# Six of eleven gate-and-up blocks as seven block products, the FFN width in three parts

## The chip, the cores and the metric

The kernel runs on one core of one Trainium2 chip. The metric is device time in microseconds for one execution; a figure for a kernel is the median of its runs. TensorE (PE) multiplies, VectorE (DVE) and ScalarE (ACT) do the elementwise work, GpSimd (POOL) a little of it, and SyncE (SP) issues most of the DMAs.

## The reference

One decoder block for 256 tokens of width 2048, all in float32:

```python
h = h + hybrid_mixer(rmsnorm(h, mix_norm_w), w_in, ...)   # projections, gated linear attention, short conv, w_out
h = h + swiglu(rmsnorm(h, ffn_norm_w), w_gate_up, w_down)
return rmsnorm(h, final_norm_w)

def swiglu(h, w_gate_up, w_down):
    gu = jnp.einsum('bsd,df->bsf', h, w_gate_up)
    gate, up = jnp.split(gu, [FFN_HIDDEN], axis=-1)        # FFN_HIDDEN = 5632
    return jnp.einsum('bsf,fd->bsd', jax.nn.silu(gate) * up, w_down)
```

Only the second line, the FFN, is computed differently by the change.

## The kernel before

Tokens stand in two tiles `t` of 128. The contraction over 2048 is cut into 16 chunks of 128 (`KC`). Weights come as a stream of pieces of 128 x 1024 elements (512 KB): for an output of 512 columns a piece holds two chunks. `load_piece` (L112) handles one: a DMA on SP into `raw` (L127), a cast on ACT into the rounded part `hi` (L128), and a subtraction on DVE, `lo = raw - hi` (L129). Each of the three has six buffers, and `take` (L144) keeps `LOOK` = 5 pieces loaded ahead of the one in use. Activations are split in the same way into `xh`, `xl` (later `hh`, `hl` and `acth`, `actl`). `mm3` (L154) makes a product of full accuracy from three matmuls: hi·lo (L156), lo·hi (L157), hi·hi (L158). A piece so gives 2 chunks x 2 token tiles x 3 = 12 matmuls of 128x128 by 128x512 (`tok_piece`, `mm_tok`). All output goes through six rotating PSUM banks (`pmm`) and two auxiliary ones (`pax`).

[...] Small jobs are put between the pieces by `later(n, fn)`, which runs `fn` after `n` more pieces.

The FFN has 11 blocks `f` of 512 hidden columns. A block takes eight pieces of the gate matrix (`fg`) and eight of the up matrix (`fu`), 192 matmuls; its gate goes through a sigmoid on ACT (L637) and a product on DVE (L638), the up part through another product (L642), and both token tiles of the result are transposed on PE (L276) and split into `acth`, `actl` (L278, L279). The width is worked in two halves, blocks 0 to 5 and 6 to 10; after each half, the down products (`dn`) of its blocks go into four or five column groups and are added to `h` (L661). The output projection (`wo`) stands ahead of the FFN; with each of its four column groups `h` is transposed, multiplied by the norm's gain and split into `hh`, `hl` (`transpose_gain`, L264 to L269). After the last down product, `finish` scales and stores each token tile.

Of the kernel before, what the change touches and what calls it, by code (L numbers as in the profile page):

```python
# [15 lines left out]
P = 128  # L16
# [27 lines left out]
def plan():  # L44
    """Every weight group in the order of its use: (key, matrix, first row, row chunks, first column, columns)."""
# [14 lines left out]
    for half, (f0, f1) in enumerate(HALVES):  # L60
# [3 lines left out]
        for n, (c0, w) in enumerate(DOWN[half]):  # L64
            groups.append((f"dn{half}_{n}", "w_dn", f0 * 512, (f1 - f0) * 4, c0, w))
# [3 lines left out]
HALVES = ((0, 6), (6, 11))  # L69
DOWN = (  # L70
    ((0, 512), (512, 512), (1024, 512), (1536, 512)),
    ((0, 512), (512, 512), (1024, 512), (1536, 256), (1792, 256)),
)


def piece_list():
    """The groups cut into pieces of PIECE elements per partition; the first two groups alternate."""
    out = []
    for key, mat, r0, nk, c0, w in plan():
        n = PIECE // w  # L80
        out.append([(key, mat, r0 + k * P, k, min(n, nk - k), c0, w) for k in range(0, nk, n)])
    first = [p for pair in zip(out[0], out[1]) for p in pair]
    return first + [p for g in out[2:] for p in g]


@with_exitstack
def block_kernel(ctx, tc, x, xt, cols_in, gkw_in, gku_in, gnw, conv_w, finw, w_in, w_out, w_gu, w_dn, out):
# [5 lines left out]
    wraw = ctx.enter_context(tc.tile_pool(name="wraw", bufs=6))  # L93
    whi = ctx.enter_context(tc.tile_pool(name="whi", bufs=6))
    wlo = ctx.enter_context(tc.tile_pool(name="wlo", bufs=6))
# [3 lines left out]
    pmm = ctx.enter_context(tc.tile_pool(name="pmm", bufs=6, space=bass.MemoryType.PSUM))  # L99
    pax = ctx.enter_context(tc.tile_pool(name="pax", bufs=2, space=bass.MemoryType.PSUM))  # L100
# [4 lines left out]
    stream = piece_list()  # L105
    at_matrix = {}
# [3 lines left out]
    pending = []  # L110

    def load_piece():  # L112
        i = count["loaded"]
        count["loaded"] += 1
        key, mat, _, k0, n, _, w = stream[i]
        j = at_matrix.get(mat, 0)
        at_matrix[mat] = j + 1
        raw = wraw.tile([P, n, w], F32, tag="raw", name="raw")
        hi = whi.tile([P, n, w], F32R, tag="hi", name="hi")
        lo = wlo.tile([P, n, w], F32R, tag="lo", name="lo")  # L120
        # the first piece in two parts, so that the products begin sooner
        step = n // 2 if i == 0 else n
        for a in range(0, n, step):
            b = a + step
            if (i, a) in hooks:
                hooks.pop((i, a))()
            nc.sync.dma_start(raw[:, a:b, :], mats[mat][j, :, a * w:b * w].rearrange("p (k c) -> p k c", c=w))  # L127
            nc.scalar.copy(hi[:, a:b, :], raw[:, a:b, :])  # L128
            nc.vector.tensor_tensor(out=lo[:, a:b, :], in0=raw[:, a:b, :], in1=hi[:, a:b, :].bitcast(F32),  # L129
                                    op=ALU.subtract)  # L130
        ready[(key, k0)] = (hi, lo, n)

    def later(delay, fn):
        """Run fn once `delay` more pieces have been used."""
        pending.append((count["tick"] + delay, fn))

    def tick():
        count["tick"] += 1
        due = [p for p in pending if p[0] <= count["tick"]]
        for p in due:  # L140
            pending.remove(p)
            p[1]()

# [10 lines left out]
    def mm3(ps, sh, sl, mh, ml, first, last):  # L154
        """ps += (sh + sl).T @ (mh + ml) without the product of the two low parts."""
# [4 lines left out]
    def tok_piece(ps, t, piece, k0, nk, ah, al):  # L160
        hi, lo, n = piece
        ts = slice(t * P, (t + 1) * P)
        for k in range(n):
            kk = k0 + k
            mm3(ps, ah[:, kk, ts], al[:, kk, ts], hi[:, k, :], lo[:, k, :], kk == 0, kk == nk - 1)

    def mm_tok(key, nk, w, ah, al):
        """Token-major product: out[t] = a[:, t].T @ w, with a's chunks stationary."""
        ps = [pmm.tile([P, w], F32, tag="mm", name=f"{key}_{t}") for t in range(NT)]
        for k0 in range(0, nk, PIECE // w):  # L170
            piece = take(key, k0)
            for t in range(NT):
                tok_piece(ps[t], t, piece, k0, nk, ah, al)
# [11 lines left out]
    def mm_cols(keys, ah, al, each=None):  # L185
        """Column-major products: out[m] = w[:, m].T @ a, with w's chunks stationary."""
        ps = {key: [pmm.tile([P, T], F32, tag="mm", name=f"{key}_{m}") for m in range(2)] for key in keys}
# [8 lines left out]
    # ---------------------------------------------------------------- constants  # L196
# [3 lines left out]
    warm = const.tile([P, 512], mybir.dt.bfloat16, name="warm")  # L200
# [4 lines left out]
    warm_ps = pax.tile([P, 512], F32, tag="ax", name="warm_ps")  # L205
# [3 lines left out]
    mix = ExitStack()  # L209
    mpool = mix.enter_context(tc.tile_pool(name="mpool", bufs=1))  # L210
    gla = ExitStack()
    gpool = gla.enter_context(tc.tile_pool(name="gpool", bufs=1))

    # the low-rank decay's down-projection: hi in columns 0:16, lo in 16:32 of one stationary operand
# [4 lines left out]
    # ---------------------------------------------------------------- x: split of x * gain, transposed  # L219
# [22 lines left out]
    # x arrives in step with the first pieces of the weights  # L242
# [7 lines left out]
    # ---------------------------------------------------------------- helpers  # L250
# [8 lines left out]
    def transpose_gain(c0, hi, lo):  # L259
        """Chunks c0, c0 + 1 of h to hi + lo = (h * gain) transposed."""  # L260
        ps = pax.tile([P, 2, T], F32, tag="ax", name="tr")
        for j in range(2):
            for t in range(NT):
                nc.tensor.transpose(out=ps[:, j, t * P:(t + 1) * P],  # L264
                                    in_=h[:, t, (c0 + j) * P:(c0 + j + 1) * P], identity=ident)
        for j in range(2):
            c = c0 + j
            nc.scalar.activation(hi[:, c, :], ps[:, j, :], AF.Copy, scale=ffc[:, c:c + 1])
            nc.vector.scalar_tensor_tensor(out=lo[:, c, :], in0=ps[:, j, :], scalar=ffc[:, c:c + 1],  # L269
                                           in1=hi[:, c, :].bitcast(F32), op0=ALU.mult, op1=ALU.subtract)  # L270

    def transpose_block(src, t, hi, lo, c0):
        """128 tokens x 512 columns to four chunks of hi + lo."""
        ps = pax.tile([P, 4, P], F32, tag="ax", name="trb")
# [7 lines left out]
    # ---------------------------------------------------------------- first products  # L282
    gk_ps = pax.tile([P, T], F32, tag="ax", name="gk_ps")
# [10 lines left out]
    mask = const.tile([P, NT, P], I8, name="mask")  # L294
    restart = const.tile([P, T], F32, name="restart")
# [3 lines left out]
    rb = const.tile([P, T], F32, name="rb")  # L299
# [12 lines left out]
    def make_constants():  # L312
# [3 lines left out]
        # mask[j, i] = 1 where j <= i, for both token tiles  # L316
        maskf = const.tile([P, P], F32, name="maskf")
# [410 lines left out]
```

## Time and profile before

| what | us |
|---|---|
| median of 3 runs (1563.91 to 1564.59) | 1564.22 |
| span of the profiled execution | 1561.5 |
| PE busy in it | 1549.7 |
| DVE busy | 859.3 |
| ACT busy | 706.4 |
| first matmul of the output projection | 732.6 |
| first gate product | 823.3 |
| first down product | 1089.9 |
| last matmul begins | 1553.7 |

The span runs from the first to the last instruction of the profiled execution; the time of a run also holds what lies around it. Busy times of PE are modelled and overlap, so the distance of the starts of two matmuls, not the duration of one, says what a matmul costs. In rows of groups, the numbers behind the bar are the total of busy time, the mean duration in ns, and the idle time of the engine just before them with what ended it.

### The profile page before, as it was taken

Reading aid. Unit: us, or ns where it says so; the run is one execution under the profiler, and the core shown is the slowest. Engines: PE = TensorE matmul, PEld = TensorE weight load, DVE = VectorE, ACT = ScalarE, POOL = GpSimd, SP = SyncE. Lnnn points to the kernel's source line nnn. Section 1 sums busy time; section 2 is a strip of 40 time slices with the busy share of each in tenths; the row PEclk is TensorE's granted clock in tenths of the full one; section 3 lists DMA queues with packets and bytes.
Section 4 is the critical chain, followed back from the end, with each engine's and each line's share of the span. In section 5 each row is a group of like instructions: output and inputs, shape, how many; then the busy total and the mean of one; then the engine's idle time right before and its main releaser. Section 6 shows DMA issues by size and latency. Waiting matters only on the chain.

```text
span 1561.5 us, 18914 instructions
## 1 busy us (share of the span) xinstructions
PE 1549.7 (99%) x7417; PEld 1304.0 (84%) x7417; DVE 859.3 (55%) x866; ACT 706.4 (45%) x797; POOL 16.6 (1%) x29
## 2 busy tenths in 40 slices
PE   9999999999999999999999999999999999999998
PEld 8989988888888888888888888888888888888887
DVE  6765546554745655665555555555544555555554
ACT  7763453444444344444445444444433444444443
POOL 0020000000000000000000000000000000000000
PEclk9999999999999999999999999999999999999999
DMA  9655567766766766666566666565666666666561
GB/s 351 208 171 170 179 194 206 231 189 204 231 191 190 242 192 190 201 213 193 188 183 215 188 190 191 189 192 189 188 192 197 190 189 189 189 195 188 189 197 68
DMA packets 86081, 306.11 MB, mean 196 GB/s; under 512 B 9740, under 2 KB 9868, under 8 KB 85864
## 3 DMA queue, kind: packets, MB, share of 16 engines
q1 hardware_dynamic: 82560, 296.02, 60.0%
q10 hardware_dynamic: 3432, 8.89, 2.3%
q8 instruction: 58, 0.95, 0.3%
q14 instruction: 31, 0.25, 0.0%
HBM read 298.60 MB, written 2.10 MB: 193 GB/s over the span
## 4 chain that ended last, share of the span: by engine, by line
PE 96%; DVE 1%; ACT 1%; issue 1%; POOL 0%; DMA 0%; SPq 0%; DVEq 0%; ACTq 0%
PE dn L158 5%; PE dn L157 5%; PE dn L156 5%; PE fg L158 5%; PE fg L156 5%; PE fg L157 5%; PE fu L158 5%; PE fu L156 5%; PE fu L157 5%; PE wo L158 2%; PE gc L156 2%; PE g L156 2%; PE gb L156 2%; PE xc L156 2%; PE wo L157 2%; PE ma L156 2%
## 5 line engine op out<-in xcount | busy, mean ns | idle before, releaser
L129 DVE TENSOR_TENSOR lo<-raw,hi 128x1024 fp32r<-128x1024 f32 (+1 forms) x553 | 674.5, 1223 | 629.6 <-ACT hi L128 629.2
L128 ACT CAST hi<-raw 128x1024 fp32r<-128x1024 f32 (+1 forms) x553 | 579.7, 1051 | 780.2 <-PE fu L158 140.0
L156 PE MATMUL dn<-lo,acth 128*128 128x512 f32 (+1 forms) x392 | 144.2, 368 | 0.0
L158 PE MATMUL dn<-hi,acth 128*128 128x512 f32 (+1 forms) x392 | 144.0, 367 | 0.0
L157 PE MATMUL dn<-hi,actl 128*128 128x512 f32 (+1 forms) x392 | 144.0, 367 | 0.0
L156 PE MATMUL fg<-lo,hh 128*128 128x512 f32 x352 | 137.8, 392 | 0.0
L158 PE MATMUL fg<-hi,hh 128*128 128x512 f32 x352 | 137.1, 389 | 0.0
L157 PE MATMUL fg<-hi,hl 128*128 128x512 f32 x352 | 137.0, 389 | 0.0
L156 PE MATMUL fu<-lo,hh 128*128 128x512 f32 x352 | 136.9, 389 | 0.0
L157 PE MATMUL fu<-hi,hl 128*128 128x512 f32 x352 | 136.9, 389 | 0.0
L158 PE MATMUL fu<-hi,hh 128*128 128x512 f32 x352 | 136.9, 389 | 0.0
L158 PEld LDWEIGHTS dn<-hi,acth 128*128 128x128 f32 x392 | 73.9, 189 | 12.2
L156 PEld LDWEIGHTS dn<-lo,acth 128*128 128x128 f32 x392 | 73.9, 189 | 12.2
L157 PEld LDWEIGHTS dn<-hi,actl 128*128 128x128 f32 x392 | 73.9, 189 | 12.1
L158 PEld LDWEIGHTS fg<-hi,hh 128*128 128x128 f32 x352 | 66.1, 188 | 13.8
L157 PEld LDWEIGHTS fu<-hi,hl 128*128 128x128 f32 x352 | 66.1, 188 | 13.7
L158 PEld LDWEIGHTS fu<-hi,hh 128*128 128x128 f32 x352 | 66.1, 188 | 13.7
L156 PEld LDWEIGHTS fu<-lo,hh 128*128 128x128 f32 x352 | 66.1, 188 | 13.7
L157 PEld LDWEIGHTS fg<-hi,hl 128*128 128x128 f32 x352 | 66.1, 188 | 13.4
L156 PEld LDWEIGHTS fg<-lo,hh 128*128 128x128 f32 x352 | 66.1, 188 | 13.4
L156 PE MATMUL v<-lo,xh 128*128 128x512 f32 x128 | 50.3, 393 | 0.0
L156 PE MATMUL wo<-lo,mh 128*128 128x512 f32 x128 | 50.2, 392 | 0.0
(201 smaller groups left out, 2487.6 us busy)
## 6 DMA issues: line engine op xcount, KB each, us to landing
raw<-in_w_in_dram SPq DMA_DIRECT2D x255, 512.0 KB, 4.2
raw<-in_w_gu_dram SPq DMA_DIRECT2D x176, 512.0 KB, 3.6
raw<-in_w_dn_dram SPq DMA_DIRECT2D x88, 512.0 KB, 3.5
raw<-in_w_out_dram SPq DMA_DIRECT2D x32, 512.0 KB, 3.7
u<-u ACTq DMA_DIRECT2D x8, 448.0 KB, 5.6
taps<-in_conv_w_dram ACTq DMA_DIRECT2D x4, 768.0 KB, 10.1
h<-in_x_dram SPq DMA_DIRECT2D x4, 512.0 KB, 9.9
xs<-in_xt_dram SPq DMA_DIRECT2D x3, 512.0 KB, 6.6
```

Source lines behind the costliest of these rows:

```text
L128: nc.scalar.copy(hi[:, a:b, :], raw[:, a:b, :])
L129: nc.vector.tensor_tensor(out=lo[:, a:b, :], in0=raw[:, a:b, :], in1=hi[:, a:b, :].bitcast(F32), op=ALU.subtract)
L156: nc.tensor.matmul(ps, lhsT=sh, rhs=ml, start=first, stop=False)
L157: nc.tensor.matmul(ps, lhsT=sl, rhs=mh, start=False, stop=False)
L158: nc.tensor.matmul(ps, lhsT=sh, rhs=mh, start=False, stop=last)
```

## The change

Six blocks (0, 2, 4, 6, 8, 10) are computed with Winograd's form of Strassen's scheme. Sixteen chunks are four quads `q` of four chunks. For a quad, the activations are a matrix of 2 x 2 blocks: two token tiles by two pairs of chunks, and the weights one of 2 x 2 blocks too: two pairs of chunks by (gate, up). Eight block products become seven, each of two chunks for one token tile: six matmuls. Their operands on the weights' side are three weight blocks as they are (called 11, 21 and 22) and four sums t1 to t4 of weight blocks, that DVE makes from float32 weights before they are split: t1 = up(0) + gate(0), t3 = up(0) + up(1), t2 = t3 + gate(0), t4 = t2 + gate(1) (signs are in the sums on the activations' side). `y` holds gate(0), `x` holds up(0) and then in turn t3, t2 and t4, in place; each has one buffer. On the activations' side four sums per quad (`sh`, `sl`) are made once, in `transpose_gain`. The seven products are accumulated over the quads in five PSUM banks (`p0_0` to `p0_4` for block 0) and joined by additions on DVE.

The other five blocks are computed as before, but with one pair of banks for gate and up in turn, and their pieces are mixed into those of the seven-product blocks by `merged`. The FFN width is worked in three parts of 4, 4 and 3 blocks; the first two column groups of the down products are worked together, block by block. Buffers of the weights are five instead of six, and `LOOK` is 4.

The diff, cut to its core:

```diff
+PARTS = ((0, 4), (4, 8), (8, 11))
+SEVEN = (0, 2, 4, 6, 8, 10)
+def seven_list(f):
+    sums = [(f"s{f}", (what, q)) for q in range(4) for what in ("11", "t1", "t3", "t2", "t4")]
+    return sums + [(f"s{f}", (what, q)) for q in range(4) for what in ("21", "22")]
+def merged(part):
...
+    sevens = [e for f in range(f0, f1) if f in SEVEN for e in seven_list(f)]
+    eights = [e for f in range(f0, f1) if f not in SEVEN for e in eight_list(f)]
...
+        total += 2 if e[1][0][0] == "t" else 1
...
+    places += [((n + 0.9) / len(eights), 1, n, e) for n, e in enumerate(eights)]
...
-    wraw = ctx.enter_context(tc.tile_pool(name="wraw", bufs=6))
+    wraw = ctx.enter_context(tc.tile_pool(name="wraw", bufs=5))
...
-    LOOK = 5
+    LOOK = 4
...
+    def sum_of(key, what, q):
+        fg, fu = key.replace("s", "fg"), key.replace("s", "fu")
+        if what == "21":
+            return fetch(fg, 4 * q + 2)
+        if what == "22":
+            return fetch(fu, 4 * q + 2)
+        if what == "11":
+            held["y"] = fetch(fg, 4 * q, dpool, "y")
+            return held["y"]
+        y = held["y"]
+        if what == "t1":
+            held["x"] = fetch(fu, 4 * q, dpool, "x")
+            raw = wraw.tile([P, 2, 512], F32, tag="raw", name="raw")
+            nc.vector.tensor_tensor(out=raw, in0=y, in1=held["x"], op=ALU.add)
+            return raw
+        other = y if what == "t2" else fetch(fu if what == "t3" else fg, 4 * q + 2)
+        x = held["x"]
+        nc.vector.tensor_tensor(out=x, in0=x, in1=other, op=ALU.add)
+        return x
...
+            raw = sum_of(key, *k0)
+            piece = split_tiles(2, 512)
+            split(raw, piece)
...
+    def transpose_gain(q, hi, lo, shi, slo):
...
+        for s, p, m in ((0, a21, a22), (1, a11, sums[:, 0]), (2, a21, a11), (3, a12, sums[:, 1])):
+            nc.vector.tensor_tensor(out=sums[:, s], in0=p, in1=m, op=ALU.subtract)
+        nc.scalar.copy(shi[:, q], sums)
+        nc.vector.tensor_tensor(out=slo[:, q], in0=sums, in1=shi[:, q].bitcast(F32), op=ALU.subtract)
...
+    def quad(ps, pair, piece, first, last):
+        hi, lo, n = piece
+        for j in range(n):
+            ah, al = pair(j)
+            mm3(ps, ah, al, hi[:, j, :], lo[:, j, :], first and j == 0, last and j == n - 1)
...
+    def sevens(f, put):
...
+        for q in range(4):
+            for ps, pair in ((pa, block_of(0, 4 * q)), (pb, sum_block(0, q)), (pd, sum_block(2, q)),
+                             (pc, sum_block(1, q)), (pe, block_of(1, 4 * q + 2))):
+                piece = yield
+                quad(ps, pair, piece, q == 0, q == 3)
...
+                if ps is pa:
+                    nc.scalar.copy(v2, pa)
+                elif ps is pc:
+                    nc.vector.tensor_tensor(out=v2, in0=pc, in1=v2, op=ALU.subtract)
+                    nc.vector.tensor_tensor(out=v3, in0=pd, in1=v2, op=ALU.add)
+                    nc.vector.tensor_tensor(out=u1, in0=pb, in1=v3, op=ALU.add)
+                elif ps is pe:
+                    nc.vector.tensor_tensor(out=g1, in0=pe, in1=v3, op=ALU.subtract)
+                    silu_gain(sg[:, 1, :], g1, 1)
+                    times(sg[:, 1, :], u1, 1)
+                    put(4, sg[:, 1, :], 1)
+        for q in range(4):
+            for ps, pair in ((pa, block_of(0, 4 * q + 2)), (pb, sum_block(3, q))):
...
+        nc.vector.tensor_tensor(out=u1, in0=pb, in1=v2, op=ALU.add)
+        times(sg[:, 0, :], u1, 0)
+        put(3, sg[:, 0, :], 0)
```

In the orders below `lo`, `hi`, `raw`, `x`, `y` and `sg` are the tiles named above, with buffer numbers.

The first place is DVE in the FFN. Before, from the pieces of the second block, after the up part of block 0 (`fu0`):

```order
L129 TENSOR_TENSOR lo_6826<-raw_6824,hi_6825 128x1024
L642 SCALAR_TENSOR_TENSOR sg_6691<-fu0_0_6696,r2_6512,sg_6691 128x512
L642 SCALAR_TENSOR_TENSOR sg_6691<-fu0_1_6697,r2_6512,sg_6691 128x512
L129 TENSOR_TENSOR lo_6848<-raw_6846,hi_6847 128x1024
L129 TENSOR_TENSOR lo_6880<-raw_6878,hi_6879 128x1024
```

Now, the second quad of block 0 with pieces of block 1 (`lo` from `raw_6650`, `raw_6682` and `raw_6724`) between:

```order
L193 TENSOR_TENSOR lo_6635<-y_6632,hi_6634 128x1024
L193 TENSOR_TENSOR lo_6652<-raw_6650,hi_6651 128x1024
L209 TENSOR_TENSOR raw_6664<-y_6632,x_6662 128x1024
L193 TENSOR_TENSOR lo_6667<-raw_6664,hi_6666 128x1024
L193 TENSOR_TENSOR lo_6684<-raw_6682,hi_6683 128x1024
L213 TENSOR_TENSOR x_6662<-x_6662,raw_6694 128x1024
L193 TENSOR_TENSOR lo_6698<-x_6662,hi_6697 128x1024
L213 TENSOR_TENSOR x_6662<-x_6662,y_6632 128x1024
L193 TENSOR_TENSOR lo_6709<-x_6662,hi_6708 128x1024
L193 TENSOR_TENSOR lo_6726<-raw_6724,hi_6725 128x1024
L213 TENSOR_TENSOR x_6662<-x_6662,raw_6736 128x1024
L193 TENSOR_TENSOR lo_6740<-x_6662,hi_6739 128x1024
```

Where subtractions stood in a row, four sums (L209, L213) now stand among them, each with the subtraction of its own result right behind it.

The second place is SP at the same point. Before:

```order
L127 DMA raw_7011<-in_w_gu_dram 128x1024
L127 DMA raw_7029<-in_w_gu_dram 128x1024
L127 DMA raw_7047<-in_w_gu_dram 128x1024
L127 DMA raw_7065<-in_w_gu_dram 128x1024
L127 DMA raw_7083<-in_w_gu_dram 128x1024
```

Now, from the last loads of one quad to the first of the next (`y_6767`, `x_6779`):

```order
L183 DMA raw_6736<-in_w_gu_dram 128x1024
L234 DMA raw_6755<-in_w_gu_dram 128x1024
L183 DMA y_6767<-in_w_gu_dram 128x1024
L183 DMA x_6779<-in_w_gu_dram 128x1024
L234 DMA raw_6799<-in_w_gu_dram 128x1024
L183 DMA raw_6811<-in_w_gu_dram 128x1024
```

The loads of `y` and `x`, which have one buffer each, stand ahead of raw loads that have five.

The third place is DVE in the third part (block 8), from one quad to the next; the row `lo_10711` is a piece of block 9:

```order
L213 TENSOR_TENSOR x_10608<-x_10608,raw_10664 128x1024
L193 TENSOR_TENSOR lo_10668<-x_10608,hi_10667 128x1024
L193 TENSOR_TENSOR lo_10680<-y_10677,hi_10679 128x1024
L209 TENSOR_TENSOR raw_10691<-y_10677,x_10689 128x1024
L193 TENSOR_TENSOR lo_10694<-raw_10691,hi_10693 128x1024
L193 TENSOR_TENSOR lo_10711<-raw_10709,hi_10710 128x1024
```

Here one subtraction stands between the last reader of the old `x` (`lo_10668`) and the first sum that reads the new one (`raw_10691`); in the first place there are two.

More of the change, by code (lines that the diff above doesn't have):

```diff
@@ L164, in tok_piece @@
             kk = k0 + k
[L165 removed]
+            mm3(ps, ah[:, kk, ts], al[:, kk, ts], hi[:, k, :], lo[:, k, :], first and k == 0, last and k == n - 1)
     def mm_tok(key, nk, w, ah, al):
[L169 removed]
+        ps = [bank([P, w], f"{key}_{t}") for t in range(NT)]
         for k0 in range(0, nk, PIECE // w):
@@ new lines, in hidden, with begin, put @@
+    def hidden(part, acth, actl):
+        f0, f1 = PARTS[part]
+        order = [f for f in range(f0, f1)]
+        going = {}
+        def begin(f):
+            def put(delay, src, t):
+                one_at_a_time(delay, lambda: transpose_act(src, t, acth, actl, 4 * (f - f0)))
+            g = (sevens if f in SEVEN else eights)(f, put)
+            next(g)
+            return g
+        for key, k0 in merged(part):
+            f = int(key.lstrip("sfgu"))
+            if f not in going:
+                going[f] = begin(f)
+            try:
+                going[f].send(take(key, k0))
+            except StopIteration:
+                pass
+            used()
```

319 lines of the change are left out of this document (210 added, 109 removed).

## The prediction

> **What bounds the kernel now.** I read the engine shares of the page first, then what ended the idle time (groups by line), then the waits of TensorE, then single rows of the timeline.
>
> ```profile
> PE 1549.7 (99%) x7417; PEld 1304.0 (84%) x7417; DVE 859.3 (55%) x866; ACT 706.4 (45%) x797; POOL 16.6 (1%) x29
> PE 96%; DVE 1%; ACT 1%; issue 1%; POOL 0%; DMA 0%; SPq 0%; DVEq 0%; ACTq 0%
> L129 DVE TENSOR_TENSOR lo<-raw,hi 128x1024 fp32r<-128x1024 f32 x551 | 673.1, 1225 | 628.5 <-ACT hi L128 628.1
> L128 ACT CAST hi<-raw 128x1024 fp32r<-128x1024 f32 x551 | 578.4, 1053 | 779.4 <-PE fu L158 140.0 <-PE dn L158 132.9 <-PE fg L158 123.4
> PE o_ps L156 <- ACT scr L456: 1.6, 1, 1.6
> ```
>
> TensorE (PE) is busy for 99% of the span and carries 96% of the chain that ended last; its longest wait for another engine is 1.6 us. The two engines that split the weights wait for it: the casts on ScalarE (ACT) were released by PE, the subtractions on VectorE (DVE) by the casts. So a matmul taken away in the FFN is worth its full pitch, as long as DVE, at 55%, doesn't become the later one. That is the question here.
>
> ```profile
> 999.67 0.39 PE L156 MATMUL fu<-lo,hh 128*128 128x512 f32 x1
> ...
> 1003.53 0.39 PE L158 MATMUL fg<-hi,hh 128*128 128x512 f32 x1
> L156 PE MATMUL fg<-lo,hh x352: 389/389/478, 823.3 to 1420.1; 128*128 128x512 f32 x176
> L156 PE MATMUL dn<-lo,acth x392: 278/389/478, 1089.9 to 1553.5; 128*128 128x512 f32 x156, 128*128 128x256 f32 x40
> ```
>
> The two timeline rows are the first and the last of 18 matmuls without a gap: 3.86/17 = 0.227 us each, whatever the modelled 0.39 says. The six blocks of the first half run from the first fg (823.3) to the first dn (1089.9): 266.6 us, 44.43 a block. That is 192 x 0.227 = 43.6 for the products and 0.83 for eight transposes. Eleven blocks: **488.8 us**.
>
> **What the change removes.** A block by seven products has 28 pieces of six matmuls instead of 16 of twelve: 168, not 192. Six blocks save 6 x 24 x 0.227 = **32.7 us** of PE. The down products keep their number, and PE stays their bound: a piece is 12 x 0.227 = 2.72 us there, against one cast and one subtraction.
>
> **What it adds.** Each seven-product block has 12 more pieces to split and 16 sums, on DVE. The sums aren't in the trace; the nearest row is a product of the same size, the two operands of which lie in SBUF as theirs do.
>
> ```profile
> L567 DVE TENSOR_TENSOR ya<-ya,on 128x1024 f32<-128x1024 f32 x4 | 4.9, 1224 | 4.5 <-ACT on L566 4.5
> 97.29 3.48 DVE L129 TENSOR_TENSOR lo<-raw,hi 128x1024 fp32r<-128x1024 f32 x3
> L638 DVE SCALAR_TENSOR_TENSOR sg<-fg,r,sg 128x512 f32<-128x512 f32 x22 | 16.4, 748 | 5.5 <-ACT sg L637 5.5
> L584 DVE TENSOR_TENSOR h<-wo,h 128x512 f32<-128x512 f32 x8 | 5.1, 682 | 0.0
> ```
>
> So a sum takes 1.225 us, like a subtraction. Three subtractions with nothing to wait for take 3.48, a pitch of 1.13 (each start overlaps the row before by 0.09); short rows (0.748 and 0.682) by the same overlap 0.66 and 0.59.
>
> A sum also has to be split before it is of use, and the order of DVE puts its subtraction right behind it, with the cast on ACT between them:
>
> ```profile
> 1001.23 1.06 ACT L128 CAST hi<-raw 128x1024 fp32r<-128x1024 f32 x1 [1.67 <-PE fu L158]
> 1002.32 1.23 DVE L129 TENSOR_TENSOR lo<-raw,hi 128x1024 fp32r<-128x1024 f32 x1 [0.17 <-ACT hi L128]
> 100.70 0.44 DVE L455 COPY_PREDICATED scr<-mask,sc_ps 128x256 f32<-128x256 int8 x1
> 101.17 0.27 ACT L456 COPY scr<-sc_ps 128x128 f32<-128x128 f32 x1 [4.12 <-DVE scr L455]
> ```
>
> A hand-over costs 0.03 us in either direction. Sum, hand-over, cast 1.05, hand-over, subtraction: DVE stands still for 1.13 us, and the overlap of 0.09 is lost too: **1.22 us a sum**, unless another row lies between. Before, DVE waits for casts as well, but a piece ahead of need; now it waits inside the work that feeds PE.
>
> Second new wait: x has one buffer. Its next load can start only when the last subtraction of the quad before has read it, and the first sum needs it.
>
> ```profile
> raw<-in_w_gu_dram SPq DMA_DIRECT2D x176, 512.0 KB, 3.6
> DMA to landing us min/median/max: 3.4/3.9/11.1
> ```
>
> A load of w_gu lands 3.6 us after its issue (3.4 at the least and 11.1 at the most, all weights). I take 3.6. Issue comes about 0.1 us after the subtraction. Behind this load SP's queue also holds the following raw loads; in the order they are wanted some 3.5 us after the first sum, so I give them no cost. What lies between on DVE is two subtractions in half of the places in parts 0 and 1 (a wait of 1.5), three in the others (0.4), and a single one in four places of part 2 (2.7).
>
> **The sum, by DVE's rows in the order.** Each of parts 0 and 1 has, from the second quad to the last sum's subtraction, 69 subtractions and 28 sums (97 x 1.13 = 109.6), 10 and 11 short rows (6.6 + 6.5), 28 cast waits of which 20 are bare, two half covered by a row of 0.59 and the rest covered (20 x 1.22 + 2 x 0.63 = 25.7), load waits 4 x 1.5 + 2 x 0.4 = 6.8, and 1.3 for sums that overwrite x right after it was read: **156 us**. The beginning: DVE is ahead when PE comes from PE-bound work, so only two evictions, two sums and four subtractions of the first quad remain, 8.3 us; in part 0 also the split of the last sums of h, two rows of 1.13, four of about 0.33 and one cast wait: 13.0. The end: from there PE is late again, with 9 pieces of 6, 3 of 12 and four transposes: 12.3 + 8.2 + 0.4 = 20.9. Part 0: 190; part 1: 185.5. Part 2 (two sevens, one eight): 56 + 28 rows (94.9), short rows 9.3, cast waits 23 x 1.22 + 0.6 = 28.7, load waits 2 x 1.5 + 4 x 2.7 = 13.8, 1.5, so 148; with 8.3 and 12.3 + 5.4 + 0.4 = 18.1: 174.5.
>
> Sum 550 against 488.8: **+61 us** instead of -32.7. What hid DVE's work until now was PE at 2.72 us for each 1.23 of DVE; a seven-product piece leaves 1.36.
>
> Small edits. Five weight buffers for six and LOOK 4 for 5 touch the dense places: the start (DMA-limited) and the decay tables (the 1.6 us wait). Between nothing, since the bound there is a load or a chain that doesn't depend on it, and one piece of 2.7 at each: I take 1. The sums of h (a few us per wo group of 8 x 2.72) fit beside PE; if that cover were gone they would cost about 5 a group. Banks: single ones for the eight blocks, covered by the pieces of the other block that lie between; uncovered, some 1.5 us twelve times. The last group is shorter but its finish is unchanged: 0.
>
> Span 1561.5 + 61.4 + 1 = 1623.9. The median of the runs, 1564.2, is 2.7 above the profiled span of 1561.5 for what lies around it: **1627 us**.
>
> **Rivals.** (1) The waits are hidden, and it isn't slower. The price of all waits is 2 x 25.7 + 28.7 + 2 x 6.8 + 13.8 = 107.5. Without any, parts 0 and 1 fall to PE's own 166.8 each (720 x 0.227 + 3.3) and part 2 to DVE's 132: 466 in all, about 1543 for the kernel; were DVE free everywhere, 1531. It turns from slower to faster once 61 of the 107 are hidden. For it: ACT has room, and the eight blocks' subtractions stand near. Against it: the order has them behind the waiting row, and this kernel shows that a waiting row holds its engine:
>
> ```profile
> 84.80 1.06 ACT L417 ACTIVATE exk<-exk 128x1024 f32<-128x1024 f32 x1 [7.41 <-POOL exk L413]
> 85.77 1.03 ACT L128 CAST hi<-raw 128x1024 fp32r<-128x1024 f32 x1
> ```
>
> The cast behind exk started without a gap, though 7.4 us had passed. [...] I give 0.12.
>
> (2) PE's clock falls in its new gaps. In four places of part 2 PE has one piece and then waits for x, sum, cast and subtraction: 4.8 us.
>
> ```profile
> 1555.00:1557.00 2.00, 0.00 (x0) 0.00 (x0) 1.58 (x4) 1.04 (x3) 0.00 (x0) 1.00 0.03 9
> 1557.00:1558.00 1.00, 0.00 (x0) 0.00 (x0) 0.00 (x0) 0.00 (x0) 0.00 (x0) 0.93 1.02 385
> 1558.00:1559.00 1.00, 0.00 (x0) 0.00 (x0) 0.00 (x0) 0.00 (x0) 0.00 (x0) 0.50 1.06 346
> ```
>
> These windows (the clock is the third number from the end) show it at 0.50 about 4 us after the last matmul (1553.5 for its first term). Were it to stay there, a quad of part 2 (5 x 1.36 + 1.5 x 2.72 = 10.9) would need 21.8 on PE against DVE's 19: seven times 2.8, about 1647. Against it: gaps that long are few, and PE has dense work between. [...] Chance 0.08.
>
> (3) The x load lands later, since its queue has just been held: 1 us more on 18 places is +18, 1645. For it the maximum of 11.1, against it 3.6 as a median. Chance 0.10.
>
> (4) That the change doesn't do what it says is excluded by the order: PE issues 168 matmuls for a block of the six.
>
> **How the numbers follow.** Forecast 0.70: 1627, its own range 1610 to 1645 (landing 3.4 to 3.9: -4 to +5; overlap lost or full on a third of the rows: +9 or -3; small edits -1 to +5). The others as priced. Without the tails below 1600 and above 1660 the range holds about 0.85. Faster by over 0.2% (what a measurement of this kernel can tell from no change): 0.10, from (1). Within: 0.02, the middle of (1). Slower: 0.88.
>
> **What would show it.** Right: PE's busy time falls by about 33 while it idles some 95 more, nearly all inside fg, fu and the p products; DVE is above 1050 us busy (859 + 96 x 1.225 + 72 x 1.225 + some 25 short rows); the subtractions of sums wait about 1.1 us each for ACT, the first sums of a quad up to 2.7 for a DMA; dn stages stay without gaps, and part 2 loses the most (+41). Wrong: if the sums' subtractions show no idle time before them, or PE's gaps end on something else than `lo` (a bank, a transpose), the ledger above is wrong there; a granted clock below 1.00 in part 2 is (2); landings above 4 us for x are (3).

## The result, and the profile after

The changed kernel takes 1652.63 us (median of 4 runs, 1651.48 to 1654.75), against 1564.21 us of the kernel before on the same chip: ratio 1.0567 [1.0552, 1.0582], **88.4 us slower**. The span of its profiled execution is 1650.8 us. The prediction was 1627 us, within 1600 to 1660: the direction and the range were right, the central value was 25.6 us low.

The first lines to read are the same as before: shares of the engines and the chain, then the groups of split and sum, the waits, and the load of x.

```profile
PE 1562.6 (95%) x7225; PEld 1285.1 (78%) x7225; DVE 1075.8 (65%) x1080; ACT 781.1 (47%) x883; POOL 17.7 (1%) x29
PE 67%; DVE 15%; DMA 6%; ACT 6%; issue 5%; POOL 1%; SPq 0%; ACTq 0%; DVEq 0%
L193 DVE TENSOR_TENSOR lo<-x,hi 128x1024 fp32r<-128x1024 f32 x72 | 88.1, 1224 | 64.3 <-ACT hi L192 64.2
L272 PE MATMUL p<-lo,sh 128*128 128x512 f32 x144 | 63.9, 444 | 47.7 <-DVE lo L193 47.6
PE p L272 <- DVE lo L193: 65.4, 53, 4.4
DVE raw L209 <- DMA x<-in_w_gu_dram: 26.1, 18, 2.7
DVE sg L771 <- ACT sg L767: 7.1, 6, 2.8
DVE v L808 <- PE p L274: 3.9, 2, 2.3
x<-in_w_gu_dram SPq DMA_DIRECT2D x24, 512.0 KB, 3.6
```

TensorE (PE) has 192 matmuls fewer (144 by the seven products, 48 because fewer of the last part's down products are cut into two of 256 columns) and still a busy time that is 13 us longer. In the third part the modelled duration of a matmul is 0.39 us in dense work, 0.50 for the first one behind a wait (1407.33), and 0.63 at a granted clock of 0.50 (1420.37 to 1422.93, starts 0.43 apart): here busy time misleads. The chain says more. PE's share fell from 96% to 67%, and VectorE (DVE), ScalarE (ACT) and DMA, which had 2% together, now have 27%. PE's longest wait for another engine was 1.6 us; now the products `p` wait 65.4 us in 53 places for `lo`. DVE is only 65% busy, but it stands behind its own sums: 64.3 us ahead of the subtractions of x, for the casts, and 26.1 us at the first sum of a quad, for the load of x.

A hidden stage is the stretch of a part from its first gate, up or `p` matmul to its first down product. A window for each of the three (columns: window, its length, busy time and number for PE, PE's weight loads, DVE, ACT, POOL; then the granted clock, DMA's share and GB/s):

```profile
825.00:1021.90 196.90, 178.40 (x753) 139.64 (x753) 159.76 (x156) 105.07 (x117) 0.00 (x0) 0.97 0.64 216
1110.10:1303.60 193.50, 174.31 (x746) 136.64 (x744) 155.95 (x148) 97.69 (x104) 0.00 (x0) 0.99 0.65 219
1391.70:1575.50 183.80, 145.76 (x542) 110.53 (x541) 133.87 (x125) 78.53 (x83) 0.00 (x0) 0.88 0.53 181
```

They take 196.9, 193.5 and 183.7 us, 574.1 together, where the eleven blocks took 487.8 before (266.6 and 221.2, from the stage starts in the trace). That is 86.3 of the 89.3 us by which the span grew. The stretch before the FFN grew by 1.7, the down products by 1.2.

The timeline shows what one step costs, at the start of the third part. DVE first, then ACT at the same time:

```profile
1392.68 1.22 DVE L213 TENSOR_TENSOR x<-x,y 128x1024 f32<-128x1024 f32 x1
1395.09 1.22 DVE L193 TENSOR_TENSOR lo<-x,hi 128x1024 fp32r<-128x1024 f32 x1 [1.19 <-ACT hi L192]
1396.35 1.23 DVE L213 TENSOR_TENSOR x<-x,raw 128x1024 f32<-128x1024 f32 x1
1398.77 1.22 DVE L193 TENSOR_TENSOR lo<-x,hi 128x1024 fp32r<-128x1024 f32 x1 [1.19 <-ACT hi L192]
1399.91 1.22 DVE L193 TENSOR_TENSOR lo<-y,hi 128x1024 fp32r<-128x1024 f32 x1
1401.04 1.22 DVE L193 TENSOR_TENSOR lo<-raw,hi 128x1024 fp32r<-128x1024 f32 x1
1403.63 1.23 DVE L209 TENSOR_TENSOR raw<-y,x 128x1024 f32<-128x1024 f32 x1 [1.37 <-DMA x<-in_w_gu_dram]
1406.05 1.23 DVE L193 TENSOR_TENSOR lo<-raw,hi 128x1024 fp32r<-128x1024 f32 x1 [1.20 <-ACT hi L192]
1407.20 1.22 DVE L213 TENSOR_TENSOR x<-x,raw 128x1024 f32<-128x1024 f32 x1
```

```profile
1394.01 1.05 ACT L192 CAST hi<-x 128x1024 fp32r<-128x1024 f32 x1 [3.70 <-DVE x L213]
1397.68 1.05 ACT L192 CAST hi<-x 128x1024 fp32r<-128x1024 f32 x1 [2.63 <-DVE x L213]
1398.64 1.05 ACT L192 CAST hi<-y 128x1024 fp32r<-128x1024 f32 x1
1399.59 1.04 ACT L192 CAST hi<-raw 128x1024 fp32r<-128x1024 f32 x1
```

The first sum ends at 1393.90, its cast starts at 1394.01, and the subtraction starts 0.03 after the cast: DVE stands for 1.19 us, and again behind the second sum. The subtractions of `y` and `raw` that follow could not fill these stops. Their casts (1398.64, 1399.59) stand behind those of the sums in ACT's queue, which itself had stood 3.70 and 2.63 us for the sums. Then they run without a gap, and the next sum waits 1.37 us for x.

Such a stop behind a sum with its own subtraction next stands in the trace 65 times, with a median of 1.19 us. In 46 of them the row behind is a subtraction whose cast comes after the sum's on ACT, and in 11 it is a sum that overwrites the x which the waiting subtraction still reads. In the other eight it is the next sum, which needs nothing of the waiting row; in four of these its data were there no later than 0.04 us after the stop began. The last rows above are one of the four: the weights of `x<-x,raw` had landed at 1404.90 (the last update of that load's semaphore in the trace), and it starts at 1407.20, behind the subtraction that waited from 1404.86 to 1406.05.

### The profile page after: what moved, and what is told of

Same layout as the page of the kernel before. It is cut to its first block, busy times and chain, and to the rows that moved or that the text cites. A ratio compares the mean times of both kernels' runs of the same rounds, so it can differ in the third digit from the quotient of the medians.

```text
span 1650.8 us, 18958 instructions
## 1 busy us (share of the span) xinstructions
PE 1562.6 (95%) x7225; PEld 1285.1 (78%) x7225; DVE 1075.8 (65%) x1080; ACT 781.1 (47%) x883; POOL 17.7 (1%) x29
## 4 chain that ended last, share of the span: by engine, by line
PE 67%; DVE 15%; DMA 6%; ACT 6%; issue 5%; POOL 1%; SPq 0%; ACTq 0%; DVEq 0%
DVE lo L193 7%; ACT hi L192 5%; PE dn L272 5%; PE dn L274 5%; PE dn L273 5%; DVE x L213 4%; DMA x<-in_w_gu_dram 4%; PE wo L272 2%; PE wo L274 2%; PE gc L273 2%; PE gc L274 2%; PE g L273 2%; PE gb L273 2%; PE xc L273 2%; PE ma L273 2%
## 5 line engine op out<-in xcount | busy, mean ns | idle before, releaser
L192 ACT CAST hi<-x 128x1024 fp32r<-128x1024 f32 x72 | 75.5, 1049 | 165.9 <-DVE x L213 152.5
L193 DVE TENSOR_TENSOR lo<-x,hi 128x1024 fp32r<-128x1024 f32 x72 | 88.1, 1224 | 64.3 <-ACT hi L192 64.2
L272 PE MATMUL p<-lo,sh 128*128 128x512 f32 x144 | 63.9, 444 | 47.7 <-DVE lo L193 47.6
L272 PEld LDWEIGHTS p<-lo,sh 128*128 128x128 f32 x144 | 28.4, 197 | 69.5 <-DVE lo L193 64.8
L272 PE MATMUL fu<-lo,hh 128*128 128x512 f32 x160 | 63.9, 399 | 4.1 <-DVE sg L771 4.1
L272 PE MATMUL fg<-lo,hh 128*128 128x512 f32 x160 | 64.8, 405 | 0.0
L273 PE MATMUL fg<-hi,hl 128*128 128x512 f32 x160 | 64.6, 404 | 0.0
L274 PE MATMUL fg<-hi,hh 128*128 128x512 f32 x160 | 64.1, 401 | 0.0
L273 PE MATMUL fu<-hi,hl 128*128 128x512 f32 x160 | 63.4, 396 | 0.0
L274 PE MATMUL fu<-hi,hh 128*128 128x512 f32 x160 | 63.2, 395 | 0.0
L274 PE MATMUL p<-hi,sh 128*128 128x512 f32 x144 | 60.7, 421 | 0.0
L213 DVE TENSOR_TENSOR x<-x,raw 128x1024 f32<-128x1024 f32 x48 | 58.6, 1221 | 2.7 <-DMA raw<-in_w_gu_dram 2.4
```

Of the source, the lines that this page charges most:

```text
L192: nc.scalar.copy(hi[:, ks, :], raw[:, ks, :])
L193: nc.vector.tensor_tensor(out=lo[:, ks, :], in0=raw[:, ks, :], in1=hi[:, ks, :].bitcast(F32), op=ALU.subtract)
L213: nc.vector.tensor_tensor(out=x, in0=x, in1=other, op=ALU.add)
L272: nc.tensor.matmul(ps, lhsT=sh, rhs=ml, start=first, stop=False)
L273: nc.tensor.matmul(ps, lhsT=sl, rhs=mh, start=False, stop=False)
L274: nc.tensor.matmul(ps, lhsT=sh, rhs=mh, start=False, stop=last)
```

## The experiments

Times are medians; ratios are to the kernel before, timed beside each on the same chip. Unless said otherwise an edit is made to the changed kernel.

**1. No seven-product blocks.** All eleven blocks by eight products, in three parts; their banks come in turn from the six rotating ones, not as the fixed pair `b5`, `ax1`.

```diff
-SEVEN = (0, 2, 4, 6, 8, 10)
+SEVEN = ()
-            ps = [bank([P, 512], f"{m}{f}_{t}", tag) for t, tag in enumerate(("b5", "ax1"))]
+            ps = [bank([P, 512], f"{m}{f}_{t}") for t in range(NT)]
```

> All eleven blocks by eight products, in three parts, with five buffers and LOOK 4; everything else as in the changed kernel. Theory A (the loss is DVE's chain of sums, casts and subtractions in the seven-product blocks): the FFN hidden stages go back to 488.8 us in all, and the kernel to about 1567 (1564.2, 1.7 before the FFN, 1 in the down parts). Rival C (buffers, LOOK or the three parts cost it): above 1590.

1566.12 us, 1.0015 [1.0005, 1.0024]. Three parts, five buffers and the sums of h cost about 2 us. The other 86.5 us belong to the seven-product blocks.

**2. The seven products without the weight sums.** The pieces t1 to t4 are split as they come from the loads, so the output is not the reference's; matmuls, casts and subtractions keep their number.

```diff
-        y = held["y"]
-        if what == "t1":
...
-        return x
+        if what == "t2":
+            return held["y"]
+        return fetch(fg if what == "t4" else fu, 4 * q + 2 * (what != "t1"))
```

> The sums of weights are left out: pieces t1 to t4 are split straight from loaded weights, so the FFN's result is not the reference's. 28 pieces a block, five banks and the joins stay. Theory A: DVE has neither sums nor their waits, PE sets the pace (166.8, 166.8 and 122.5 us for the three hidden stages), about 1535 us (1530 to 1550). Rival B (28 small pieces, joins, banks and the clock cost it, not the sums): above 1600.

1538.1 us, 0.9837 [0.9823, 0.9852]. The 96 sums, with what waits for them, are worth 1652.6 - 1538.1 = 114.5 us; without them the change is 26 us faster. In the first two stages (window rows as above) PE is busy all the time, in the third it isn't:

```profile
825.50:992.60 167.10, 167.10 (x753) 138.00 (x752) 128.17 (x127) 107.54 (x117) 0.00 (x0) 1.00 0.78 251
1080.80:1246.80 166.00, 166.00 (x746) 137.31 (x744) 124.45 (x119) 100.55 (x104) 0.00 (x0) 1.00 0.79 253
1334.90:1462.00 127.10, 122.23 (x541) 99.83 (x540) 96.28 (x95) 78.08 (x83) 0.00 (x0) 1.00 0.77 255
```

167.1 and 166.0 agree with the prediction's 166.8. Against experiment 1 the matmuls saved bring 28.0 of the 32.7 us predicted; the rest is close to the 4.9 us (127.1 - 122.2) in which PE stands still in the third part.

**3. x free sooner.** The sum t4 is written into the weight buffer it was made from.

```diff
+        out = other if what == "t4" else x
-        nc.vector.tensor_tensor(out=x, in0=x, in1=other, op=ALU.add)
-        return x
+        nc.vector.tensor_tensor(out=out, in0=x, in1=other, op=ALU.add)
+        return out
```

> The sum t4 is written over the weights loaded for it, not over x. x is free earlier, and t2 and t4 can be summed one after the other, so that each covers the other's cast. By the ledger of DVE's rows load waits fall from 27 to 5 us and cast waits from 85 to 41: Theory A 1590 (1575 to 1600). If only the load wait counts: about 1625. Rival B: above 1645.

1579.92 us, 1.0104 [1.0089, 1.0119]: 72.7 us won back with the same 96 sums, so the sums' busy time by itself is not what the 88 us are made of. The edit also changed the build order: fewer sums have their own subtraction next (the table behind experiment 12).

**4. Filler for the clock.** In the third part, from the second quad on, matmuls with a stationary tile of zeros are added ahead of each product of a quad, ten ahead of the second (`pb`) and three ahead of the others, so that PE doesn't stand still so long.

```diff
+    zero = const.tile([P, P], F32R, name="zero")
+    nc.vector.memset(zero.bitcast(F32), 0.0)
+    filler = hh[:, 0:2, :].rearrange("p k t -> p (k t)")
...
                 piece = yield
+                if f >= 8 and q:
+                    for j in range(10 if ps is pb else 3):
+                        nc.tensor.matmul(ps, lhsT=zero, rhs=filler, start=False, stop=False,
+                                         skip_group_check=True)
```

> In the third part 3 or 10 matmuls with a stationary tile of zeros are added ahead of each waiting product, from the second quad on, so that PE is not idle there; they add nothing to the sums. If the falls of the granted clock are on the path, the third hidden stage gets shorter by 5 to 8 us and the kernel takes about 1646; if PE's spare time covers them, it stays at 1652; if the filler is in the way, it gets longer.

```profile
1391.60:1574.10 182.50, 164.03 (x673) 129.03 (x672) 133.77 (x125) 78.96 (x83) 0.00 (x0) 0.95 0.54 182
```

1651.82 us (1651.59 to 1653.49). The granted clock of the third part rose from 0.88 to 0.95, the time fell by 0.8 us, inside the spread of the runs. So the clock was lower with the gaps than with filler in them, as rival (2) had it, but more than half of what was missing in it was worth no more than 0.8 us: PE's spare time covered the rest.

**5. Transposes two pieces later.** From the subtraction of a part's last sum to its first down product the trace has 23.3, 23.7 and 20.0 us; the prediction had 20.9, 20.9 and 18.1. PE stands there ahead of transposes (`trb`).

```diff
-                    put(2, sg[:, t, :], t)
+                    put(4, sg[:, t, :], t)
-                    put(4, sg[:, 1, :], 1)
+                    put(6, sg[:, 1, :], 1)
-        put(3, sg[:, 0, :], 0)
+        put(5, sg[:, 0, :], 0)
```

> Edit to the changed kernel: the transposes of the hidden activations are put two pieces later (delays 2, 3, 4 become 4, 5, 6), nothing else. In the changed kernel the stretch from the last sum's subtraction to the first down product takes 23.3, 23.7 and 20.0 us, where the prediction had 20.9, 20.9 and 18.1, and TensorE stands twice in it, 1.2 and 0.9 us, ahead of a transpose whose operand waits for a sigmoid. Theory A (transposes come too early behind a late sigmoid): these stretches shrink to about 21, and the kernel to 1646 us (1644 to 1649). Rival B (the stretch is held by the late weight loads in front of the sigmoid, so another wait takes over): within 1.5 us of the changed kernel.

1649.59 us (1649.42 to 1653.05), 1.0551 [1.0536, 1.0567]; the interval overlaps that of the changed kernel. This lies between the two expectations and settles neither. The trace of the changed kernel shows why moving a transpose helps little. ACT, DVE and PE in the second part:

```profile
1286.52 1.05 ACT L192 CAST hi<-raw 128x1024 fp32r<-128x1024 f32 x1 [3.22 <-DMA raw<-in_w_gu_dram]
1287.47 0.72 ACT L767 ACTIVATE sg<-g,r 128x512 f32<-128x512 f32 x1
```

```profile
1288.23 0.75 DVE L771 SCALAR_TENSOR_TENSOR sg<-g,r,sg 128x512 f32<-128x512 f32 x1 [1.50 <-ACT sg L767]
1288.90 1.22 DVE L193 TENSOR_TENSOR lo<-raw,hi 128x1024 fp32r<-128x1024 f32 x1
1290.03 0.75 DVE L771 SCALAR_TENSOR_TENSOR sg<-u,r,sg 128x512 f32<-128x512 f32 x1
```

```profile
1290.92 0.63 PE L403 MATMUL trb<-ident,sg 128*128 128x128 f32 x4 [1.29 <-DVE sg L771]
```

A cast waits 3.22 us for a late weight load, the sigmoid starts behind it on ACT (its `g` was there at 1285.60), the two products behind that on DVE (1.50 us), the transposes behind those on PE (1.29 us): one wait through four queues. With the transposes later, PE still stood at the first of them, in the first two parts (1.0 and 1.9 us).

**6. The sums taken out of x** ("v1"). t3 and t4 go into the weight buffers, t2 into x.

```diff
-        other = y if what == "t2" else fetch(fu if what == "t3" else fg, 4 * q + 2)
         x = held["x"]
-        nc.vector.tensor_tensor(out=x, in0=x, in1=other, op=ALU.add)
-        return x
+        if what == "t2":
+            nc.vector.tensor_tensor(out=x, in0=held.pop("t3"), in1=y, op=ALU.add)
+            return x
+        raw = fetch(fu if what == "t3" else fg, 4 * q + 2)
+        nc.vector.tensor_tensor(out=raw, in0=raw, in1=x, op=ALU.add)
+        if what == "t3":
+            held["t3"] = raw
+        return raw
```

> Edit: x keeps up(0) as fetched; t3 and t4 are written into the fetched weight buffers, t2 = t3 + gate(0) into x. Same 96 sums, same casts and subtractions. x is free after the sum that makes t4, and t3's sum no longer has to wait for the subtraction of t2's chain. Theory A (in-order waits of VectorE: a sum, its cast, its subtraction, and the x load behind the last subtraction): cast waits fall from about 26, 26 and 30 us a part to 9, 5 and 12, load waits from 8, 5 and 13 to 0, 3 and 3; VectorE's rows then fill 166, 162 and 148 us a part, where TensorE's own matmuls need 166.8 in the first two: 1562 us (1555 to 1572). Rival B (VectorE's added busy time alone is what counts, waits are only where the time shows): no better than the kernel with t4 alone moved, 1580.

1562.55 us, 0.9989 [0.998, 0.9999]. As expected by the theory of the waits; the 90 us are gone with every sum still there. The stages take 170.4, 167.1 and 143.6 us. From the stage start to the last sum's subtraction, DVE's waits for casts add up to 28.0 us and those for x to 3.5 (82.8 and 26.0 in the changed kernel; the table behind experiment 12).

**7. As 6, and each sum a piece ahead of its split** ("v2").

```diff
-            raw = sum_of(key, *k0)
+            raw = summed.pop(i) if i in summed else sum_of(key, *k0)
+            for j in range(i + 1, min(i + 3, len(stream))):
+                if j not in summed and isinstance(stream[j][1], tuple) and stream[j][1][0][0] == "t":
+                    summed[j] = sum_of(stream[j][0], *stream[j][1])
+                    break
...
```

> Edit: as the run before, and each sum is issued ahead of the split of the piece before it, so that a subtraction lies between a sum and its own subtraction and the cast is covered. The same instructions in another order. Theory A: cast waits 2.5, 1.4 and 5.5 us a part; the first two parts at TensorE's own 166.8, the third at VectorE's 144: 1554 us (1548 to 1562). Rival B (busy time counts, not the order): the same as the run before.

1559.83 us, 0.9973 [0.9962, 0.9984]: inside the expected 1548 to 1562, but only 2.7 us below experiment 6 where 8.5 were expected, and the third stage is a miss. The first two stages stand at PE's bound (168.0, 166.2), but the third takes 145.9, no less than in 6, although only 7 of 96 sums have their own subtraction next in the program, where 6 has 18. DVE's waits for casts did not fall either: 27.9 us in the same stretches, where the expectation had 9.4.

**8. As 7, with a second buffer for y.** In 7, SyncE's queue stood in the third part for the sum that reads y last (columns: total, times, longest). The second fence is SyncE's queue in this run, in the third part.

```profile
SPq L184 <- DVE x L214: 44.7, 5, 10.7
```

```profile
1426.19 0.33 SPq L190 DMA_DIRECT2D y<-in_w_gu_dram  x1
1430.69 0.33 SPq L190 DMA_DIRECT2D x<-in_w_gu_dram  x1
1431.07 0.42 SPq L190 DMA_DIRECT2D raw<-in_w_gu_dram  x1
1431.54 0.42 SPq L252 DMA_DIRECT2D raw<-in_w_gu_dram  x1
```

> Edit to the kernel with the sums a piece ahead (six seven-product blocks): y gets a second buffer, nothing else. In that kernel the third part takes 145.9 us where TensorE's own matmuls need 122; SyncE's queue stands there 44.7 us behind y's buffer in five places, and ScalarE's casts 16.6 us for weights that come late. Theory A (the load of y holds the queue, and with it the weights behind): the third part falls to 125 to 135, the kernel to 1539 to 1550 us. Rival B (VectorE's rows and waits, 120 + 17 us, hold it): 1556 to 1561 us.

1559.39 us, 0.9967 [0.9953, 0.9981]: no gain, as its rival (1556 to 1561) had it. The load of x stands in the queue right behind that of y and holds back the same weight loads: they go out at once when x does, 4.5 us after y. No run has x and y with two buffers each, and what holds six seven-product blocks at 1559 us stays open.

**9. As 7, with five seven-product blocks.** The third part has one instead of two.

```diff
-SEVEN = (0, 2, 4, 6, 8, 10)
+SEVEN = (0, 2, 4, 6, 8)
```

> Edit: as the run before, with five seven-product blocks instead of six (0, 2, 4, 6, 8), so that the third part has one seven-product and two eight-product blocks. TensorE's own time there is 127 + 24 x 0.227 = 132.4 us, VectorE's rows about 76 x 1.14 + 10 = 97 and its waits. Theory A: the third part goes from 144 to 133, 1543 us (1538 to 1552), faster than both kernels. Rival B (something else than VectorE's queue holds the third part, loads or the clock): no gain against the run before, or 5 us slower by the matmuls that come back.

```profile
PE 1524.0 (99%) x7249; PEld 1278.1 (83%) x7249; DVE 1038.0 (68%) x1047; ACT 774.4 (50%) x870; POOL 17.7 (1%) x29
825.90:993.30 167.40, 167.40 (x754) 138.02 (x752) 156.09 (x155) 106.45 (x117) 0.00 (x0) 1.00 0.75 254
1081.50:1247.50 166.00, 166.00 (x746) 137.25 (x744) 152.90 (x147) 99.90 (x104) 0.00 (x0) 1.00 0.75 255
1335.70:1462.60 126.90, 126.90 (x570) 105.11 (x568) 99.03 (x93) 68.75 (x70) 0.00 (x0) 1.00 0.70 225
```

**1539.78 us, 0.9845 [0.9831, 0.986]**: faster than both kernels, with PE busy through all three stages. The third takes 126.9 us with 24 matmuls more than in 7, less than the 133 expected: that figure added them to the 127.1 us of experiment 2, which hold 4.9 us of standing still. Against experiment 1 the saving is 26.3 us, where five blocks of 24 matmuls are worth 5 x 24 x 0.227 = 27.2.

**10. A second buffer for x**, nothing else.

> Edit to the changed kernel: x gets a second buffer, nothing else. Theory A (the prediction's term for the x load): the waits of the first sum of a quad for its load, 8.0, 5.0 and 13.0 us in the three parts of the profile, with 18 times 0.08 of lost overlap, go: 1652.6 - 27.4 = 1625 us (1620 to 1632), and the half-clock spells of the third part become fewer, since TensorE's long gaps stood behind that load. Rival B (another load or a weight buffer is late there too and takes its place): less than half of it, above 1638 us.

1583.19 us, 1.0119 [1.0104, 1.0134]: 69.4 us less instead of 27.4. The waits for x went, 26 us as expected, but with them nearly half of the waits for casts (82.8 to 44.2). The timeline shows how:

```profile
L199 DVE TENSOR_TENSOR lo<-x,hi 128x1024 fp32r<-128x1024 f32 x72 | 88.1, 1224 | 45.1 <-ACT hi L198 44.4
```

```profile
925.23 1.22 DVE L219 TENSOR_TENSOR x<-x,raw 128x1024 f32<-128x1024 f32 x1
926.36 0.68 DVE L412 TENSOR_TENSOR actl<-trb,acth 128x512 fp32r<-128x512 f32 x1
926.96 1.22 DVE L215 TENSOR_TENSOR raw<-y,x 128x1024 f32<-128x1024 f32 x1
928.10 1.22 DVE L199 TENSOR_TENSOR lo<-x,hi 128x1024 fp32r<-128x1024 f32 x1
```

The next quad's first sum now stands between the last sum and its subtraction and covers the cast. The second buffer let the tile framework arrange DVE's rows otherwise at build time: 29 of 96 sums have their own subtraction next, not 65. So this run doesn't price the load alone, which the next but one does.

**11. The cast of each sum twice**, into the same tile.

```diff
+            if k0[0][0] == "t":
+                nc.scalar.copy(piece[0], raw)
             split(raw, piece)
```

> Edit to the changed kernel: the rounded part of a sum is cast twice into the same tile, 96 more casts on ScalarE, nothing more on VectorE (whose rows keep their number; 52 sums instead of 65 have their own subtraction directly behind them, 21 instead of 7 have one row between). Theory A (VectorE stands for the cast behind each sum): a second cast adds 0.95 us (two casts in a row take 1.99 in the profile) to each directly followed sum and to each with one row between: 52 x 2.22 + 21 x 1.05 = 137 us of waits instead of 65 x 1.27 + 7 x 0.1 = 83, so 1652.6 + 54 = 1707 us (1690 to 1725). Rival B (other rows cover the cast, VectorE's busy time is what costs): within 15 us of the changed kernel.

1763.31 us, 1.1274 [1.1257, 1.1291]: 110.7 us more, twice what was expected. In 52 of the 96 places ACT has another piece's cast between the two:

```profile
906.14 1.05 ACT L224 CAST hi<-x 128x1024 fp32r<-128x1024 f32 x1
907.10 1.05 ACT L192 CAST hi<-raw 128x1024 fp32r<-128x1024 f32 x1
908.04 1.05 ACT L192 CAST hi<-x 128x1024 fp32r<-128x1024 f32 x1
```

**12. The load of x twice**, the rows of DVE in the same order.

```diff
-        nc.sync.dma_start(raw, mats[mat][j].rearrange("p (k c) -> p k c", c=w))
+        for _ in range(2 if tag == "x" else 1):
+            nc.sync.dma_start(raw, mats[mat][j].rearrange("p (k c) -> p k c", c=w))
```

> Edit to the changed kernel: each load of x is issued twice into the same tile; the order of the rows on VectorE is the same, row for row. Theory A (the first sum of a quad stands for this load in all 18 places with a wait, 26.1 us in the profile): each place waits longer by what the second load lands later; with 0.4 us more of issue and 1 to 2 us of a second 512 KB, 1.5 us: 18 x 1.5 = 27, 1680 us (1668 to 1700), and more half-clock time in the third part. Rival B (the wait is shared with the weights behind it in the queue, so only part of it counts): below 1664 us.

```profile
L210 DVE TENSOR_TENSOR raw<-y,x 128x1024 f32<-128x1024 f32 x24 | 29.4, 1224 | 91.3 <-DMA x<-in_w_gu_dram 91.2
839.58 3.96 SPq L184 DMA_DIRECT2D x<-in_w_gu_dram  x2
```

1720.52 us, 1.0998 [1.0979, 1.1016]: 67.9 us more, above the expected range. The two issues lie 3.6 us apart (3.96 less one issue of 0.33), about what such a load takes to land in this run (3.7 in the median of 48). So x came some 3.6 us later in each of 18 places (18 x 3.6 = 64.8), not the 1.5 that had been estimated: waits up by 65.1, time up by 67.9.

**The waits and the time.** For 10 to 12 and 3, DVE's waits were added up in each part from the start of the hidden stage to the subtraction of the last sum, from the rows of the timeline, in us. "Next" is the number of sums with their own subtraction directly behind them.

| kernel | next | for casts | for x | both, against changed | time, against changed |
|---|---|---|---|---|---|
| changed | 65 | 82.8 | 26.0 | 0 | 0 |
| cast twice | 52 | 193.7 | 26.8 | +111.7 | +110.7 |
| x loaded twice | 65 | 84.3 | 91.2 | +66.7 | +67.9 |
| x free sooner | 32 | 47.8 | 2.0 | -59.0 | -72.7 |
| x in two buffers | 29 | 44.2 | 1.7 (for y) | -62.9 | -69.4 |

Where waits were added, each us of them was about a us of the kernel (111.7 of waits and 110.7 of time, 66.7 and 67.9). Where they were taken away, 6 to 14 us more went with them. The table leaves out the overlap that a stop costs DVE (0.08 us in the median of 132 subtractions in a row in the changed kernel), and the short waits behind sigmoids and joins, 9.1 us in the changed kernel, 0.7 with x free sooner and 4.1 with two buffers for x.

## Why the prediction was right, and where it was short

1652.6 us lies in the stated range, but above the forecast's own one of 1610 to 1645, and near the prices of rivals (2) and (3), 1647 and 1645. The total alone would not have told them apart; the rows and runs do. The mechanism was right, and three terms of the sum were too small.

- **PE gives way to DVE.** Shown: without sums 0.984 of the time before, with them 1.057. PE's bound of 166.8 us for four blocks stands at 167.1 and 166.0.
- **Each sum costs DVE's queue its cast.** Shown by experiment 11, in which the added casts came back in full. Experiment 6 shows the other direction, with the load waits mixed in: with sums written elsewhere and ordered otherwise the 90 us were gone.
- **Rival (1), the waits are hidden,** did not occur. Before, only a row of ACT, the cast behind `exk`, showed a waiting row that holds its engine. For DVE the sum at 1407.20 shows it, 2.30 us behind its data. The twelve rows that the program has for DVE in the second quad of block 0 also stand in the trace in that order, from 837.21 to 856.78, through stops of 1.18 to 1.49 us. But stops with a ready row behind them are few, 4 of 65 for certain and at most 8: mostly the row behind is not ready, since ACT's queue has its cast behind the sum's. The program of experiment 6 hid most of them (82.8 us for casts became 28.0); no run shows the machine doing it.
- **The load of x.** Predicted 27.4 us; measured 26.0 and 18 overlaps of 0.08 lost, 27.4. By part 8.0, 5.0 and 13.0 against 6.8, 6.8 and 13.8. Landing 3.6, as taken; the issue of x comes 0.03 us behind the subtraction, where 0.1 was taken.
- **The cast wait was mis-sized: +8.8 us.** The step "Sum, hand-over, cast 1.05, hand-over, subtraction" took 0.03 us for a hand-over both ways. From cast to subtraction it is 0.03, from sum to cast 0.11 in the median of the 65 bare stops. A bare stop is 1.19 and 0.08 of overlap, 1.27 instead of 1.22; and there were 65 of them where 63 had been counted. 82.8 and 76 overlaps of 0.08 make 88.9, against 80.1.
- **The ends of the parts were mis-sized: +7.1 us** (2.4, 2.8, 1.9). The count of pieces was right; PE's stops at transposes behind late weight loads were not in it, though the prediction named a gap that ends on a transpose as a sign against its ledger. Experiment 5 didn't remove them, so their cause is read from the trace, not shown by a run.
- **Short rows were taken to wait for nothing: +8.5 us.** In the stretches of the table the product behind the sigmoid waited 0.9, 2.8 and 0.9, and the joining of the products (L808) 3.9 us in two places of the third part, 2.1 and 0.8 us after stretches of 6.8 and 10.2 us in which PE's granted clock was 0.50.
- **The rest is small.** Before the FFN +1.7 instead of +1; down products +1.2 instead of 0; around the span 1.8 instead of 2.7. In all 8.8 + 7.1 + 8.5 + 0.7 + 1.2 - 0.9 = 25.4 of the 25.6. What is left are terms of at most 1 us that happen to cancel: the old blocks took 487.8 and not 488.8, and 1626.6 was rounded to 1627.
- **Rival (2)**, the clock, occurred (0.88 in the third part) without its price of 20 us: experiment 4 took away 0.07 of the missing 0.12 of the clock there and gave back 0.8 us; the two late joins (the 3.9 us above) may be its work, which no run shows. **Rival (3)** did not occur: x landed in 3.6.
- **A sign named wrongly**: "PE's busy time falls by about 33". It rose by 13, with modelled durations of 0.50 us behind waits and 0.63 at half clock instead of 0.39. The other signs (DVE over 1050, stops of about 1.1, x waits up to 2.7, the third part losing most) are in the profile.

## What to carry to other kernels

An engine at 65% can be the bound, as DVE was here: add up the stops in its own queue, not only its work, wherever it makes an operand, hands it to another engine and needs it back. The cure cost no instruction here: another row between the two, and a result written where it doesn't hold back the next load. Experiment 6 did both at once for 90 us; more rows between, in 7, brought 2.7 us on top. Saved matmuls were worth nearly their full pitch once the helper's queue had room for them (26.3 of 27.2 us in 9); the mix of blocks is a size to tune (five sevens gave 1539.8 us, six 1559.8).

## What the runs showed that was not expected

- A second buffer for one tile moved the build order on another engine: 65 sums with their own subtraction next became 29, worth more than the load it was meant for.
- A halved clock came in stretches of multiples of 3.41 us in the clock's record of the changed kernel: eight of 3.4 to 10.2 us, 44 us in all, in the third part. Experiment 4 took away more than half of the missing clock there and gained 0.8 us.
- In experiment 12 two loads into one tile ran one after the other (3.6 us between the issues), which made the doubled load a clean way to price a wait.
